# A macaron decoder layer on one Trainium2 core: four more raw slots for the paired products, low parts of w_out on VectorE, the residual through GpSimd's queue

## The chip, the cores and the metric

The kernel runs on one NeuronCore of a Trainium2 chip. The metric is the device time of one execution in microseconds; less is better. A program's matrix products run on TensorE (PE; its weight loads are listed as PEld), elementwise work on VectorE (DVE), ScalarE (ACT) and GpSimd (POOL). Transfers are issued by instructions in the order of an engine's queue: here SyncE (SP) issues most of them, and GpSimd those that add to what lies at the target or that gather. All run on the core's 16 DMA engines.

## The reference

One decoder layer in float32 on 512 prompt tokens and 8 x 4 sample tokens (544 columns), model width 1024, hidden width 2816. Two half-step feed-forward networks (FFNs) enclose a mixer with attention heads and recurrent heads; `project`, `moba_*` and `hgrn2_chunked` are left out here, as the change touches none of their work:

```python
def swiglu(x, w_gate, w_up, w_down):
    return (jax.nn.silu(x @ w_gate) * (x @ w_up)) @ w_down
...
        yp = yp + 0.5 * swiglu(rms_norm(yp, ffn1_norm[l]), ffn1_gate[l], ffn1_up[l], ffn1_down[l])
...
        qa, ka, va, qb, kb, ib, lf, gb = project(rms_norm(yp, mix_norm[l]), w_in[l], q_norm[l],
                                                 k_norm[l], lower_bounds[l])
        attn = moba_prompt(qa, ka, va, rel_bias_table)
        rec, s_fin = hgrn2_chunked(qb, kb, ib, lf, s0)
        yp = yp + merge_groups(attn, rec, gb, hgrn_out_norm[l], w_out[l])
...
        yp = yp + 0.5 * swiglu(rms_norm(yp, ffn2_norm[l]), ffn2_gate[l], ffn2_up[l], ffn2_down[l])
```

The sample tokens take the same path with caches of keys, values and states.

## The kernel before

**Split products.** Activations lie transposed, eight tiles of 128 model rows by 544 columns, which are worked on in two halves of 272. Each float32 factor is split into a high part in TensorE's format fp32r and a low part, the difference; a product is three matrix products (high by high, high by low, low by high) added up in PSUM (`products`, line 702). One output tile of 128 rows is a column; a plain column with 8 row tiles has 8 x 2 x 3 = 48 matrix products.

**Weights.** `weight_jobs` (504) lists all weight columns in the order in which they are used: ffn1, w_in, w_out, ffn2. A plain column is loaded in two parts of 128x512 (256 KB). `w_load` (583) gives each source the next free raw slot (`room`, 552) and issues its load on SP; there are four raw slots, tile `raw`. `w_split` (620) makes high and low part in one of six weight slots (`whi`, `wlo`) and gives the raw slot back. `split_unit` (608) has two ways for the low part: ScalarE's cast for the high part and a subtraction on VectorE, or, with `transfer`, a second pass of ScalarE that writes the source negated and rounded and an accumulating transfer on GpSimd's queue that adds the source onto it and reads the raw slot until it has landed. The transfer way is used for all of w_in and w_out (the job's flag `mixer`) and for the second part of the first five gate and up columns of an FFN. `w_pump` (662) splits up to 4 units ahead, 6 where the job has the flag `mixer`.

**Paired columns.** From column f = 5 on (`NREG`, 53), gate and up of an FFN are made together by seven products in place of eight (`paired_gemm` 739, `hidden_paired` 905): 7 units x 4 row tiles x 3 = 84 matrix products. The job has five sources: half of gate, half of up, their sum (made by GpSimd in a raw slot, no load), the other half of up and the other half of gate; the second half of up is also added onto the first by an accumulating transfer. Each unit is split like a plain one. The evacuations between the products run on ScalarE and VectorE, among them ScalarE's copies into `t_g` and `sq`. At column 5, `ffn` (960) adds ten raw slots and three weight slots for paired columns by `more_slots` (568): the tiles xh0 to xl4, which hold the split activations of the plain columns until then.

**From the mixer to ffn2.** `mix` (1835) ends with the first two columns of w_out, in four PSUM buffers. `ffn2` (1902) opens a new memory pool where the mixer's was, loads the residual from DRAM into its eight tiles y (1907), adds the two columns that are made and makes the other six by `gemm` (712), which has three PSUM buffers of the kind `mm`; an addition to y gives a buffer back. `norm_add` (815) then squares and sums y, on GpSimd for tiles 1 to 6.

**What sets the order.** The order of each engine's instructions is written by a planner at build time (`Order`, 258): it gives every instruction a planned start from costs of its own and sorts by it. Instructions that are recorded before a pool closes come ahead of those recorded after. On the chip each engine takes its instructions in this order and waits where an operand isn't ready. All are recorded through one helper, so that every row of the trace bears line 288; tiles tell them apart.

Of the kernel before, what the change touches and what calls it, by code (L numbers as in the profile page):

```python
# [21 lines left out]
KD = D // 128  # L22
# [28 lines left out]
MIXED = (4, 5, 6, 0, 1, 2, 3, 7)  # L51
OVER, TICK, WARM_COLUMNS = 0.0112, 3.413, 3060
NREG = 5
AHEAD = 4
AHEAD_MIX = 6
PACE = 1.1
# [408 lines left out]
class Build:  # L465
# [38 lines left out]
    def weight_jobs(self):  # L504
        a, out = self.a, []

        def quarters(m, nk, r0, c0):
            h = nk // 2
            return [m[128 * r:128 * (r + h), c0:c0 + 128].rearrange("(k p) m -> p k m", p=128)
                    for r in (r0, r0 + h)]  # L510

        def turns(m, nk, r0, c0):
            rows = m[128 * r0:128 * (r0 + nk), c0:c0 + 128].rearrange("(k two p) m -> two p k m", two=2, p=128)
            return [rows[0], rows[1]]

        def job(kind, src, nk):
            out.append({"kind": kind, "src": src, "nk": nk // 2, "raw": [], "done": 0, "paired": kind is not None, "mixer": False})

        def plain(m, nk, r0, c0, mixer=False, start=False):
            job(None, quarters(m, nk, r0, c0), nk)  # L520
            out[-1]["mixer"] = mixer
            out[-1]["start"] = start

        def paired(kind, nk, a11, a12, a21, a22, transfer):
            job(kind, [a11, a21, a21 if transfer else None, a22, a12], nk)
            out[-1]["transfer"] = transfer

        def ffn(p, pairs):
            gate, up, down = (a[p + n][0] for n in ("_gate", "_up", "_down"))
            for g0, ng in FGROUPS[pairs]:  # L530
                for f in range(g0, g0 + ng):
                    if f < NREG:
                        plain(gate, KD, 0, 128 * f, start=True)
                        plain(up, KD, 0, 128 * f, start=True)
                    else:
                        paired("a", KD, *quarters(gate, KD, 0, 128 * f), *quarters(up, KD, 0, 128 * f), pairs)
                for m in range(0, KD, 2):
                    if pairs:
                        paired("a", ng, *turns(down, ng, g0, 128 * m), *turns(down, ng, g0, 128 * (m + 1)), True)
                    else:  # L540
                        plain(down, ng, g0, 128 * m)
                        plain(down, ng, g0, 128 * (m + 1))

        ffn("ffn1", False)
        for n, j in IN_ORDER:
            plain(a["w_in"][0], KD, 0, COLS[n] + 128 * j, True)
        for m in range(KD):
            plain(a["w_out"][0], KD, 0, 128 * m, True)
        ffn("ffn2", False)
        return out  # L550

# [110 lines left out]
    def w_pump(self):  # L662
        def ahead():
            mixer = self.splitting < len(self.jobs) and self.jobs[self.splitting]["mixer"]
            return len(self.units) < (AHEAD_MIX if mixer else AHEAD)

# [293 lines left out]
    def ffn(self, pool, wide, home, x, xg, done, pairs, first=None):  # L960
        nc = self.nc
        self.pairs, self.sums, self.hidden_raw = pairs, wide, (pool, "t_h")
        for g0, ng in FGROUPS[pairs]:
            last = g0 + ng == NFF
            hs = []
            for f in range(g0, g0 + ng):
                if f >= NREG:
                    if f == NREG:
                        yield from self.settle()
                        yield lambda: len(self.xw) == KD // 2  # L970
                        self.more_slots("a", home, [f"{t}{i}" for i in range(5) for t in ("xh", "xl")],
                                        [(f"xh{i}", f"xl{i}") for i in range(5, KD)])
                        self.w_pump()
                    yield from self.paired_gemm(self.xw, KD // 2, self.hidden_paired(pool, f - g0, hs))
                    continue
                gate, up = self.hidden(pool, f - g0, hs)
                if f == 0 and first:
                    for evac, src in zip((gate, up), first):
                        for h in range(2):
                            self.later.append(lambda e=evac, s=src, h=h: e(s[h], h))  # L980
                    continue
                yield from self.gemm(xg, KD, gate, both=f == 0)
                yield from self.gemm(xg, KD, up)
            if pairs:
                for m in range(0, KD, 2):
                    yield from self.paired_gemm(hs, ng // 2, self.down_paired(pool, x, m, done if last else lambda m: None))
                continue
            yield from self.settle()
            if last:
                self.fewer_slots()  # L990
            for m in range(KD):

                def add(p, h, m=m, last=last):
                    c = self.cols(h)
                    nc.vector.scalar_tensor_tensor(x[m][:, c], p, 0.5, x[m][:, c], op0=ALU.mult, op1=ALU.add)
                    if h and last:
                        done(m)

                yield from self.gemm(hs, ng, add, both=m == 0)
        if pairs:  # L1000
            self.fewer_slots()
# [900 lines left out]
    def ffn2(self, xspill):  # L1902
        nc = self.nc
        with self.pool("ffn2") as pool:
            x = [pool.tile([128, T], F32, name=f"y{k}") for k in range(KD)]
            for k in range(KD):
                nc.sync.dma_start(x[k], xspill[k])
            xg = []
            for m in range(KD):

                def add(p, h, m=m):
                    c = self.cols(h)
                    nc.vector.tensor_tensor(x[m][:, c], p, x[m][:, c], op=ALU.add)
                    if h:
                        xg.append(self.split_x(x[m], m, self.gains[:, 2, m:m + 1], pool))
                        self.norm_add(m, x[m])

                if m < 2:
                    for h in range(2):
                        add(self.wo[m][1][h][:, :HT], h)  # L1920
                else:
                    yield from self.gemm(self.mixed, KD, add, self.mix_order)
            self.R = None
            self.order.spawn(self.norm())
            out = self.o["y_prompt"][0].rearrange("(i p) d -> p i d", p=128)
            out_s = self.o["y_sample"].rearrange("b t d -> (b t) d")

            def store(m):
                yield
                y = self.tl(pool, [128, 4, 128], "yt", bufs=2)  # L1930
                ys = self.tl(pool, [NS, 128], "t_s", bufs=2)
                self.to_tokens(x[m], y, ys)
                nc.sync.dma_start(out[:, :, 128 * m:128 * m + 128], y)
                nc.sync.dma_start(out_s[:, 128 * m:128 * m + 128], ys)
                self.stored += 1

            self.stored = 0
            homes = [(self.xp, f"{t}{i}") for i in range(KD) for t in ("xh", "xl")] + [(pool, f"hw{i}") for i in range(5)]
            self.hidden_home, self.staging = lambda i: homes[i], 12
            self.order.spawn(self.right_factors(pool, x, 2))  # L1940
            yield from self.ffn(pool, pool, pool, x, xg, lambda m: self.order.spawn(store(m)), False)
            yield lambda: self.stored == KD
# [41 lines left out]
```

## Time and profile before

| | |
|---|---|
| median of 3 runs | 1221.71 us |
| lowest and highest | 1219.51, 1222.38 us |
| the profiled execution | 1219.56 us |
| its span, first to last instruction | 1217.8 us |
| TensorE busy | 1180.5 us, 97% of the span |
| VectorE, ScalarE, GpSimd busy | 780.5, 600.8, 281.8 us |
| bytes moved | 177.26 MB, 146 GB/s on the mean |

Where ffn1 lies is about 0 to 402 us, the mixer to 781, ffn2 with the rest of w_out behind it. In the rows an instruction reads: start, duration, engine, line, operation, output<-inputs, shapes, count; in brackets how long its engine had been idle and what ended that. An engine ending in q is its queue for transfers. Matmul records are pipelined, so neighbours overlap; the time of a column is read from start to start.

### The profile page before, as it was taken

How to read it: one execution, taken by the hardware profiler on the slowest of the kernel's cores; microseconds unless marked ns; L12 is line 12 of the kernel's file. 1: busy time of each engine (PE TensorE's matmuls, PEld its weight loads, DVE VectorE, ACT ScalarE, POOL GpSimd, SP SyncE). 2: the span in 40 equal slices, each digit the busy share in tenths (PEclk: the TensorE clock that was granted, in tenths of full speed). 3: DMA queues.
4: the chain of work that ended last, by engine and by line, in shares of the span. 5: the costliest groups of instructions: out<-in, count | busy, mean ns of one | idle time of the engine just before them, and what ended most of it. 6: DMA issues, size and time to landing. Idle time of an engine off the chain costs nothing.

```text
span 1217.8 us, 26505 instructions
## 1 busy us (share of the span) xinstructions
PE 1180.5 (97%) x10571; PEld 1117.7 (92%) x10571; DVE 780.5 (64%) x1662; ACT 600.8 (49%) x1223; POOL 281.8 (23%) x293
## 2 busy tenths in 40 slices
PE   8999999999999989999999999699989999999998
PEld 8989999999999988889888777599989999999998
DVE  5888458854775377875675357237767478845853
ACT  6645246532555446666556533255544255514642
POOL 4121021101103541213354446141110011101000
PEclk9999999999999989999999999799989999999999
DMA  6566444453325984755787988565455334533232
GB/s 171 130 168 161 127 134 120 124 139 79 87 66 153 223 214 116 174 122 133 225 230 205 277 282 272 124 158 120 118 153 157 86 87 122 142 102 87 53 110 69
DMA packets 234607, 177.26 MB, mean 146 GB/s; under 512 B 14019, under 2 KB 206051, under 8 KB 234484
## 3 DMA queue, kind: packets, MB, share of 16 engines
q1 hardware_dynamic: 206740, 108.83, 30.8%
q0 software_dynamic: 27648, 66.60, 23.8%
q8 instruction: 83, 1.36, 0.5%
q14 instruction: 40, 0.33, 0.1%
q10 hardware_dynamic: 96, 0.14, 0.0%
HBM read 133.94 MB, written 11.83 MB: 120 GB/s over the span
## 4 chain that ended last, share of the span: by engine, by line
PE 85%; DVE 5%; DMA 4%; issue 3%; ACT 1%; POOL 1%; SPq 0%; POOLq 0%; ACTq 0%; DVEq 0%
PE mm L288 58%; PE sm L288 27%; DMA wlo<-raw 1%; DMA raw<-ffn_gate 1%; DMA raw<-w_in 1%; DMA SC<-rsample 0%; DMA xin<-x_prompt 0%; DVE ms_qk L288 0%; DVE wlo L288 0%; DVE xl L288 0%; SPq L288 0%; POOL wlo L288 0%; DVE t_qk L288 0%; ACT sq L288 0%; POOL KV L288 0%
## 5 line engine op out<-in xcount | busy, mean ns | idle before, releaser
L288 PE MATMUL mm<-xh,whi 128*128 128x272 f32 x1216 | 364.5, 300 | 11.1 <-DVE y L288 9.2
L288 PE MATMUL mm<-xl,whi 128*128 128x272 f32 x1216 | 352.6, 290 | 2.0 <-DVE xl L288 1.9
L288 PE MATMUL mm<-xh,wlo 128*128 128x272 f32 x1216 | 352.5, 290 | 0.1
L288 ACT CAST whi<-raw 128x512 fp32r<-128x512 f32 (+1 forms) x256 | 154.5, 606 | 224.5 <-PE mm L288 160.5
L288 PEld LDWEIGHTS mm<-xh,whi 128*128 128x128 f32 x1216 | 231.6, 190 | 26.8 <-issue 13.6
L288 PEld LDWEIGHTS mm<-xl,whi 128*128 128x128 f32 x1216 | 231.3, 190 | 3.1 <-DVE xl L288 3.0
L288 PEld LDWEIGHTS mm<-xh,wlo 128*128 128x128 f32 x1216 | 231.1, 190 | 0.4 <-issue 0.4
L288 DVE TENSOR_TENSOR wlo<-raw,whi 128x512 fp32r<-128x512 f32 (+1 forms) x166 | 113.4, 690 | 61.9 <-ACT whi L288 59.1
L288 PE MATMUL mm<-hw,whi 128*128 128x272 f32 x704 | 132.3, 288 | 0.0
L288 POOL DMA_DIRECT2D wlo<-raw x90 | 81.3, 931 | 218.2 <-ACT wlo L288 181.8
L288 PE MATMUL sm<-xw,whi 128*128 128x272 f32 x648 | 124.3, 290 | 0.4 <-ACT t_g L288 0.4
L288 PE MATMUL mm<-xw,whi 128*128 128x272 f32 x648 | 123.2, 288 | 0.8 <-ACT t_g L288 0.8
L288 PEld LDWEIGHTS mm<-hw,whi 128*128 128x128 f32 x704 | 110.2, 188 | 0.2 <-issue 0.2
L288 PEld LDWEIGHTS sm<-xw,whi 128*128 128x128 f32 x648 | 102.8, 190 | 0.6 <-ACT t_g L288 0.6
L288 PEld LDWEIGHTS mm<-xw,whi 128*128 128x128 f32 x648 | 101.9, 189 | 1.0 <-ACT t_g L288 1.0
L288 PE MATMUL mm<-hw,wlo 128*128 128x272 f32 x352 | 101.2, 287 | 0.0
L288 PE MATMUL sm<-xw,wlo 128*128 128x272 f32 x324 | 94.0, 290 | 0.0
L288 PE MATMUL mm<-xw,wlo 128*128 128x272 f32 x324 | 93.3, 288 | 0.0
L288 PEld LDWEIGHTS mm<-hw,wlo 128*128 128x128 f32 x352 | 66.3, 188 | 0.0
L288 PE MATMUL sm<-xw,xh 128*128 128x272 f32 x304 | 60.6, 295 | 3.0 <-ACT sq L288 3.0
L288 PEld LDWEIGHTS sm<-xw,wlo 128*128 128x128 f32 x324 | 61.7, 190 | 0.2
L288 PE MATMUL mm<-xw,xh 128*128 128x272 f32 x304 | 59.7, 292 | 2.1 <-ACT sq L288 2.1
(324 smaller groups left out, 2163.4 us busy)
## 6 DMA issues: line engine op xcount, KB each, us to landing
wlo<-raw POOLq DMA_DIRECT2D x90, 256.0 KB, 4.0
raw<-ffn_down SPq DMA_DIRECT2D x64, 256.0 KB
raw<-w_in SPq DMA_DIRECT2D x56, 256.0 KB
raw<-ffn_gate SPq DMA_DIRECT2D x38, 256.0 KB
raw<-ffn_up SPq DMA_DIRECT2D x36, 256.0 KB
xl<-ffn_up SPq DMA_DIRECT2D x28, 256.0 KB
xh<-ffn_gate SPq DMA_DIRECT2D x26, 256.0 KB
xh<-ffn_up SPq DMA_DIRECT2D x24, 256.0 KB
```

The lines of the kernel that those rows point to most:

```text
L288: call(*map(real, args), **{k: real(v) for k, v in kw.items()})
```

## The change

Three edits. At the beginning of each FFN, four raw slots (`rawx0` to `rawx3`) are added that only paired jobs can take; they lie in ffn1's pool `wide` and in ffn2's own pool and stay until the ten others are given up too. The eight w_out columns lose the flag `mixer`: their 16 low parts are made by VectorE's subtraction, and the units that may be split ahead while they are next are 4, not 6. The eight residual loads are issued on GpSimd's queue, not SP's.

```diff
@@ -51,6 +51,7 @@
 NREG = 5
+NX = 4
 AHEAD = 4
@@ -545,7 +546,7 @@
         for m in range(KD):
-            plain(a["w_out"][0], KD, 0, 128 * m, True)
+            plain(a["w_out"][0], KD, 0, 128 * m)
         ffn("ffn2", False)
@@ -960,6 +961,7 @@
     def ffn(self, pool, wide, home, x, xg, done, pairs, first=None):
         nc = self.nc
         self.pairs, self.sums, self.hidden_raw = pairs, wide, (pool, "t_h")
+        self.more_slots("a", wide, [f"rawx{i}" for i in range(NX)], [])
         for g0, ng in FGROUPS[pairs]:
@@ -1904,7 +1906,7 @@
             for k in range(KD):
-                nc.sync.dma_start(x[k], xspill[k])
+                nc.gpsimd.dma_start(x[k], xspill[k])
             xg = []
```

## Rows read from the trace of the kernel before

**Rows 1.** The page, part 1: busy us, share, instructions of each engine

```profile
PE 1180.5 (97%) x10571; PEld 1117.7 (92%) x10571; DVE 780.5 (64%) x1662; ACT 600.8 (49%) x1223; POOL 281.8 (23%) x293
```

**Rows 2.** Waits of PE, whole span: total us, times, longest us

```profile
PE mm L288 <- DVE y L288: 9.2, 1, 9.2
PE sm L288 <- ACT sq L288: 3.0, 1, 3.0
...
PE mm L288 <- ACT sq L288: 2.1, 1, 2.1
```

**Rows 3.** The chain that ended last: start us, us, what

```profile
83.40 3.96 DMA raw<-ffn_gate
...
166.42 10.55 PE sm L288 x84
...
891.87 5.59 DMA raw<-ffn_gate
```

**Rows 4.** Stretches: us, busy us of PE, PEld, DVE, ACT, POOL, granted clock, DMA

```profile
78.87:94.81 15.94, 12.89 (x86) 11.99 (x85) 10.34 (x15) 7.51 (x16) 4.33 (x4) 0.89 0.81 218
720.00:755.00 35.00, 34.48 (x653) 28.79 (x647) 25.32 (x74) 18.04 (x52) 21.09 (x22) 1.00 0.90 269
755.00:771.20 16.20, 11.89 (x114) 9.26 (x113) 12.31 (x33) 3.23 (x6) 0.90 (x1) 0.79 0.38 126
781.11:795.57 14.46, 5.31 (x26) 5.15 (x25) 3.41 (x7) 2.80 (x5) 1.01 (x1) 0.65 0.86 241
888.45:907.71 19.26, 15.34 (x87) 14.43 (x86) 10.81 (x16) 7.42 (x16) 4.32 (x4) 0.74 0.79 202
```

**Rows 5.** SP's queue from 780 to 900 in order of time

```profile
779.95 5.63 SPq L288 DMA_DIRECT2D raw<-w_out  x3
785.87 4.25 SPq L288 DMA_DIRECT2D y<-xs  x8
```

**Rows 6.** Waits of SP's queue from 770 to 800: total us, times, longest us

```profile
SPq L288 <- DMA wlo<-raw: 31.8, 5, 14.2
```

**Rows 7.** GpSimd and VectorE from 770 to 800 in order of time

```profile
775.11 0.99 POOL L288 DMA_DIRECT2D wlo<-raw  x1 [19.22 <-ACT wlo L288]
...
779.35 1.73 POOL L288 DMA_DIRECT2D wlo<-raw  x2 [1.85 <-ACT whi L288]
794.56 1.40 POOL L288 TENSOR_TENSOR sqsum<-sqsum,sq 128x544 f32<-128x544 f32 x1 [13.47 <-ACT sq L288]
...
770.38 0.72 DVE L288 TENSOR_TENSOR xl<-rec,xh 128x544 fp32r<-128x544 f32 x1
```

**Rows 8.** Instructions on tile wlo: count, ns min/median/max, first and last start

```profile
L288 DVE TENSOR_TENSOR wlo<-raw,whi x166: 557/684/1692, 8.9 to 1198.1; 128x512 fp32r<-128x512 f32 x134, 128x384 fp32r<-128x384 f32 x32
...
L288 POOL DMA_DIRECT2D wlo<-raw x90: 851/874/1502, 25.3 to 874.2; - x90
```

**Rows 9.** Instructions on tile y, in the same form

```profile
L288 DVE TENSOR_TENSOR y<-mm,y x14: 430/441/443, 789.9 to 826.0; 128x272 f32<-128x272 f32 x14
L288 SPq DMA_DIRECT2D y<-xs x8: 339/431/749, 785.9 to 789.4; - x8
```

**Rows 10.** The page, part 6: DMA issues, KB each, median us to landing

```profile
wlo<-raw POOLq DMA_DIRECT2D x90, 256.0 KB, 4.0
```

**Rows 11.** Groups of GpSimd's instructions from 720 to 755: busy us, mean ns, idle before

```profile
L288 POOL DMA_DIRECT2D wlo<-raw x6 | 5.6, 941 | 7.3 <-ACT wlo L288 7.1 <-issue 0.2
```

**Rows 12.** SP's queue before the first paired columns of ffn1 and ffn2

```profile
58.72 0.38 SPq L288 DMA_DIRECT2D raw<-ffn_up  x1
...
78.67 0.37 SPq L288 DMA_DIRECT2D raw<-ffn_gate  x1
...
862.10 2.59 SPq L288 DMA_DIRECT2D raw<-ffn_up  x2
```

**Rows 13.** ScalarE in the first paired column of ffn2

```profile
897.54 0.62 ACT L288 CAST whi<-raw 128x512 fp32r<-128x512 f32 x1 [4.05 <-DMA raw<-ffn_gate]
```

**Rows 14.** GpSimd ahead of the first paired column of ffn1

```profile
69.87 1.86 POOL L288 TENSOR_TENSOR raw<-raw,raw 128x512 f32<-128x512 f32 x1 [3.61 <-DVE wlo L288]
```

## The prediction, made before the changed kernel ran

> **What bounds the kernel now.** I read the page first, then who TensorE waited for, then a table of stretches around those waits, then the queues behind them. By the page TensorE is busy for 1180.5 of 1217.8 us, 97% [rows 1]. So the kernel is bound by TensorE's products, and an edit away from TensorE pays only where TensorE stands still, or where its clock is low because it stood still. There are few such places. Of all its waits the longest is one of 9.2 us on the residual tile y, and next stand one of 3.0 us and one of 2.1 us, both on ScalarE's copy into sq [rows 2].
>
> The stretches give what each place costs. A paired column is 84 products and takes 10.55 us where nothing disturbs it [rows 3], 0.1256 us a product. The first paired column of ffn1 takes from 78.87 to 94.81, 15.94 us, which is 5.4 us too long (call it place A). That of ffn2 takes from 888.45 to 907.71, 19.26 us, 8.7 us too long (place B); the granted clock is 0.74 on its mean, so a good part of it ran at the lower of TensorE's two levels (1.2 of 2.4 GHz), which came behind the 3.0 us wait [rows 4]. The second half of output column 2 of w_out takes from 781.11 to 795.57, 14.46 us for 24 products that need 24 x 0.1256 = 3.0 us: 11.4 us too long (place C); its clock is 0.65 on the mean, behind the 9.2 us wait [rows 4]. Together 25.5 us, about all that the changed lines can reach.
>
> **Place C: the y loads and w_out.** TensorE needs a PSUM buffer that VectorE frees by adding y0, so y0's landing ends the stall. The eight loads y<-xs stand on SP's queue behind three loads of w_out sources that need 5.63 us, and go out at 785.87 [rows 5]. Why those are late: in this stretch SP waits five times, 31.8 us in all, on DMA wlo<-raw, the accumulating transfer that makes a low part and holds its source until it has landed [rows 6]. What y0 itself needs is the mixer's memory. The mixer's last VectorE instruction is xl<-rec at 770.38, over at 771.1 [rows 7]: SP's queue costs y0 about 14.8 us.
>
> After the change y0 stands on GpSimd's queue. In the kernel before GpSimd has been idle for 19.22 us when it issues wlo<-raw at 775.11; three more such issues follow, the last two at 779.35, and then nothing until 794.56 [rows 7]. The second part of the change takes just these four away. So I place the first issue at about 771.2. An issue by GpSimd takes 0.874 us at the median [rows 8], one on SP took 0.431 [rows 9]; the nearest price for the way from issue to landing is the 4.0 us of wlo<-raw, 256 KB against y's 272 [rows 10]. y0 lands at 771.2 + 0.9 + 4.0 = 776.1, and two additions of 0.441 us [rows 9] end at 777. TensorE wants the buffer at 781.1. This leaves 4 us, and more if y0 waits only for the tile whose place it takes and not for the whole mixer's memory. y1 to y7 follow at 0.9 us each, faster than a column of 48 products (6.0 us) uses them. Behind the loads on GpSimd wait the sums of squares (the one at 794.56 and five like it); nobody needs these before the norm. All 11.4 us go: bounds 9.2 (the wait alone, the slow clock staying) to 11.4, and I take 11.3, as TensorE then meets no wait before a fall of the clock.
>
> By the Trainium skill (DMA: Bandwidth & Descriptors, section Issuing engines are not separate DMA queues) the issuing engine does not matter, as all transfers run on the same 16 engines and only issue time is saved. The trace here shows another thing, a transfer stuck behind waiting ones on the same queue; by that rule place C would give nothing and the sum below 12.1 us for 23.4 (the second rival has its time).
>
> The w_out low parts: 16 pairs of a ScalarE pass and a GpSimd issue become 16 subtractions on VectorE at 0.684 us [rows 8]. Ten of them lie from 775 on. There VectorE had nothing to do from 771.1 to 789.9, and later a column of 6.0 us holds two additions (0.88 us), the split of y and now two subtractions (1.37 us): nothing on the path. The sources come free 0.68 us after the cast rather than after a pass, an issue and a landing of 4.0 us, so SP's next loads go out earlier. The other six stand from 720 to 755 [rows 11], beside the last recurrent head, whose steps keep VectorE busy for 25.32 of 35 us there and for 12.31 of the next 16.2 us [rows 4]. At worst all six delay that chain: 6 x 0.684 = 4.1 us. At best gaps take them, and GpSimd's cache gathers, which stand between the six issues of 0.941 us, end sooner by two of these, a gain of 1.9. Between -1.9 and 4.1 I take a loss of 1.0, near the middle, as VectorE's share there, 0.72, lies between free and full. If the waiting limit for units ahead falls from 6 to 4, six weight slots with two in use leave four anyhow: nothing.
>
> **Places A and B: four more raw slots.** A paired column needs five sources. Before the change it has the four ordinary slots, and the ten further ones (xh, xl) are inputs of the last plain product and free only as TensorE passes it. In ffn1 the last source of a plain column goes out at 58.72, and in ffn2 the last two by 864.69, but in ffn1 the fifth source of the first paired column only at 78.67 [rows 12], and the first source of the second paired column at 83.40. The chain that ended last runs through this very load, and in ffn2 through the one at 891.87, which took 5.59 us [rows 3]. ScalarE takes its instructions in order: its cast at 897.54 waited 4.05 us for that load [rows 13], and behind it in its order stands the copy into sq, for which TensorE waits [rows 2].
>
> With the change the first four sources go to the new slots, unused so far, directly behind the last plain load: about 59 in ffn1, about 865 in ffn2. GpSimd's sum for this column, which takes no load but a slot, waits until 69.87 for a plain split to give one back [rows 14]; so by about 70 the ordinary slots of ffn1 are free again, and by the same pattern by about 877 those of ffn2, and they take the fifth source and the second column's first three. TensorE asks for the first column at 78.87 and 888.45 and for the second 10.55 us later: against landings of 4 to 5.6 us the loads are ahead by 9 us or more. The sums on GpSimd and its accumulating transfer per column move with them, in the same number; ahead of them in GpSimd's order stand the low parts of the last plain column, which could lose one issue (0.9 us) and have 3 us to spare. The work on ScalarE and VectorE is the same and holds in every later paired column at 10.55 us. What is late next is a cast that waits for a weight slot, as in any column. I leave 0.5 us at each place for a short wait without a fall of the clock: 4.9 us at A and 8.2 at B. Bounds: nothing (the wait only moves to the next source) and all 5.4 and 8.7. The rest of each FFN runs at full pace already, and gains nothing.
>
> **The sum.** 11.3 + 4.9 + 8.2 - 1.0 = 23.4 us. The profiled execution took 1219.56 us (span 1217.8); this gives 1196.2. The median of the runs shown, 1221.71, is 2.1 us above it, so I forecast 1198.3, with 1191 to 1204 as its own range: the order of the mixer's instructions is laid out anew by the planner, and I allow 4 us either way, which no row prices, besides the bounds above.
>
> **The rivals.** First: the paired columns wait still. ScalarE's order is fixed beforehand, and a cast that waits there for any late source holds the copies again; the clock falls after short waits too (0.89 on the mean at A, with waits of 2.1 and less [rows 2, 4]). For it speaks that the planner's place for a cast rests on planned landings; against it the lead of 9 us. Half of 13.1 us stays: 1204.9. Chance 0.16.
>
> Second: y still comes late, since GpSimd's queue is held by something that I don't see or the mixer's memory is given back as a whole later than 771.1. A and B stay: 1198.3 + 11.3 = 1209.6. Against it stands GpSimd's empty queue. Chance 0.09.
>
> Third: the new slots are not used early, as loads are issued in a planned order, and C also stays: 1218 to 1222, chance 0.05.
>
> Fourth, slower: VectorE becomes the bound of the mixer's end. The six subtractions go between the recurrent head's steps, TensorE gets waits of about 3 us there, and its clock falls as it does behind the 3.0 us wait of place B. From 720 to 755 it now works nearly without a gap, 34.48 of 35 us at a clock of 1.00 [rows 4]; at the lower level this is up to 34 us more, and 1198.3 + 34 = 1232. [...] Chance 0.04.
>
> **How the numbers follow.** Forecast 0.64; better than its range 0.02. Differences of 0.3%, 3.7 us, are about what a measurement of this kernel tells from none. Faster: 0.64 + 0.02 + 0.16 + 0.09 = 0.91; same 0.05; slower 0.04. The range 1190 to 1208 holds the forecast, the first rival and a little of the second, some 0.83.
>
> **What would show it.** TensorE's list of waits without the 9.2 us on y and without sq; y<-xs issued by GpSimd within a microsecond or two of the mixer's last VectorE instruction; the fifth gate source issued some 10 us before the first paired column starts; both such columns near 10.6 us with a clock of 1.00. Wrong would be a wait of y on another queue, a cast waiting for raw<-ffn_gate in those columns, or new gaps of TensorE between the last heads.

## The result, and the profile after

The changed kernel takes 1205.64 us (1204.40 to 1207.49) where the kernel before takes 1222.05 us (1219.51 to 1223.85) beside it: ratio 0.9868, 95% interval 0.9845 to 0.9892, so 13 to 19 us less. It is faster, by 16.4 us of the medians, and 7 us above the forecast of 1198.3: inside the range of 1190 to 1208 that took in the first rival, outside the forecast's own of 1191 to 1204. Its profiled execution took 1206.72 us (span 1204.9), 12.84 us less than that of before (1219.56), where the sum had 23.4.

Who TensorE waited for in the changed kernel over the whole span (total us, times, longest us), as in [rows 2]; its rows bear line 289:

```profile
PE sm L289 <- issue: 4.0, 11, 0.8
PE mm L289 <- DVE xl L289: 3.8, 3, 2.2
...
PE mm L289 <- ACT sq L289: 2.1, 1, 2.1
...
PE mm L289 <- DVE t_h L289: 1.5, 2, 1.2
...
PE mm L289 <- DVE wlo L289: 1.3, 1, 1.3
```

The 9.2 us on y and the 3.0 us on sq are gone; there is still one of 2.1 us on sq, in the same column as before (place A). The stretches of the changed kernel say the same (columns as in [rows 4]): the first and the second paired column of ffn1, from its last paired column through the mixer to column 2 of w_out, from there to the first paired column of ffn2, and that column:

```profile
80.77:97.20 16.43, 12.76 (x87) 12.14 (x85) 12.82 (x17) 6.67 (x14) 6.57 (x6) 0.90 0.90 228
97.20:108.94 11.74, 11.26 (x86) 10.67 (x85) 10.40 (x20) 8.06 (x17) 0.00 (x0) 1.00 0.45 118
354.50:785.32 430.82, 416.46 (x4582) 358.64 (x4581) 272.10 (x728) 225.50 (x512) 157.69 (x174) 0.99 0.69 188
785.32:883.97 98.65, 98.59 (x791) 98.37 (x789) 68.79 (x144) 50.87 (x90) 21.41 (x21) 1.00 0.54 139
883.97:894.51 10.54, 10.54 (x86) 10.54 (x85) 8.52 (x13) 6.97 (x15) 4.79 (x4) 1.00 1.14 292
```

With the same stretches of before the account of the two profiled executions is:

| stretch | before | after | change | forecast |
|---|---|---|---|---|
| start of the first paired column of ffn1 | 78.87 | 80.77 | +1.90 | |
| that column (place A) | 15.94 | 16.43 | +0.49 | |
| the second one | 10.66 | 11.74 | +1.08 | |
| from the third to the last of ffn1 | 245.98 | 245.56 | -0.42 | A in all: -4.9, came +3.05 |
| mixer, to column 2 of w_out | 426.65 | 430.82 | +4.17 | +1.0 |
| to the first paired column of ffn2 (C) | 110.35 | 98.65 | -11.70 | -11.3 |
| that column and the next (B) | 29.85 | 21.39 | -8.46 | -8.2 |

So places B and C came in the size that was forecast, place A became a loss, and the mixer got longer. These two differences, 8.0 and 3.2 us, are what is missing.

**Where place A went.** SP's queue and GpSimd of the changed kernel in the plain columns of ffn1, in order of time:

```profile
32.06 0.45 SPq L289 DMA_DIRECT2D rawx<-ffn_gate  x1
32.56 1.05 SPq L289 DMA_DIRECT2D rawx<-ffn_up  x2
...
44.58 0.38 SPq L289 DMA_DIRECT2D raw<-ffn_gate  x1
```

```profile
37.08 1.87 POOL L289 TENSOR_TENSOR rawx<-rawx,rawx 128x512 f32<-128x512 f32 x1 [9.46 <-DMA rawx<-ffn_up]
...
40.06 2.06 POOL L289 DMA_DIRECT2D wlo<-raw  x2
```

The sources of column 5 go out at 32 us, in the middle of the plain columns, not at 59. GpSimd takes its instructions in order, so its sum waits 9.46 us for these loads, and behind it stand two low parts of a plain column; their raw slots come free late, the gate load behind them goes out at 44.58 (the same load in the kernel before, in the row below, at 38.02), and TensorE waits 1.33 us for a low part at 50.83; by the first paired column it is 1.9 us behind.

```profile
38.02 0.38 SPq L288 DMA_DIRECT2D raw<-ffn_gate  x1
```

The code says why 32 us: the planner gives a tile that was never used the opening of its pool as its earliest time (`self.order.touched[name] = self.since`, line 176), and puts its load into the first gap of SP's plan.

In the first paired column itself, the second cause, on SP's queue, ScalarE and TensorE:

```profile
83.64 1.36 SPq L289 DMA_DIRECT2D rawx<-ffn_up  x1
```

```profile
89.46 0.62 ACT L289 CAST whi<-rawx 128x512 fp32r<-128x512 f32 x1 [4.72 <-DMA rawx<-ffn_up]
89.98 0.38 ACT L289 COPY sq<-mm 128x272 f32<-128x272 f32 x1
```

```profile
90.41 0.52 PE L289 MATMUL mm<-xw,xh 128*128 128x272 f32 x2 [2.14 <-ACT sq L289]
```

A source of the second column was given an extra slot that comes free late; its load stands behind eight loads into the tiles xh and xl (a column has four loads) and goes out at 83.64, the cast waits 4.72 us for it, and the copy into sq behind the cast holds TensorE for 2.14 us. It is the picture of [rows 13], with the next source. The column is 5.9 us too long; 1.5 us more are waits on VectorE's t_h, and the granted clock is 0.90 on its mean.

### The profile page after: what moved, and what is told of

It is laid out like the page before. It is cut to its first block, busy times and chain, and to the rows that moved or that the text cites. A ratio compares the mean times of both kernels' runs of the same rounds, so it can differ in the third digit from the quotient of the medians.

```text
span 1204.9 us, 26484 instructions
## 1 busy us (share of the span) xinstructions
PE 1175.7 (98%) x10571; PEld 1112.3 (92%) x10571; DVE 793.0 (66%) x1678; ACT 593.4 (49%) x1207; POOL 270.6 (22%) x285
## 4 chain that ended last, share of the span: by engine, by line
PE 84%; DVE 5%; DMA 4%; ACT 2%; issue 2%; POOL 2%; SPq 0%; POOLq 0%; ACTq 0%; DVEq 0%
PE mm L289 57%; PE sm L289 27%; DMA SC<-rsample 1%; DMA rawx<-ffn_up 1%; DMA wlo<-raw 1%; DMA xl<-ffn_up 1%; ACT xh L289 1%; DVE wlo L289 1%; ACT sq L289 1%; DMA xin<-x_prompt 0%; POOL sqsum L289 0%; ACT whi L289 0%; DVE xl L289 0%; DMA raw<-w_in 0%; DVE raw L289 0%
## 5 line engine op out<-in xcount | busy, mean ns | idle before, releaser
L289 ACT CAST whi<-raw 128x512 fp32r<-128x512 f32 (+1 forms) x242 | 146.0, 605 | 225.2 <-PE mm L289 176.6
L289 DVE TENSOR_TENSOR wlo<-raw,whi 128x512 fp32r<-128x512 f32 (+1 forms) x168 | 116.7, 700 | 57.7 <-ACT whi L289 55.1
L289 POOL DMA_DIRECT2D wlo<-raw x74 | 67.1, 936 | 175.7 <-ACT wlo L289 141.4
L289 PEld LDWEIGHTS mm<-xw,wlo 128*128 128x128 f32 x324 | 61.0, 188 | 0.0
```

Source lines behind the costliest of these rows:

```text
L289: call(*map(real, args), **{k: real(v) for k, v in kw.items()})
```

## The experiments

The kernels ran on several chips, on which the kernel before has medians of 1218.6 to 1224.6 us; so times are compared by their ratio to the kernel before on the same chip, and stretches, which are sharper, by the profiles. Several edits work on loads of ffn1 alone, whose job numbers are below 60 (`self.loading`); number 10 is the first paired column.

**The slots in ffn2 alone**

```diff
-        self.more_slots("a", wide, [f"rawx{i}" for i in range(NX)], [])
+        if pool is wide:
+            self.more_slots("a", wide, [f"rawx{i}" for i in range(NX)], [])
```

> The change, but with the four extra slots opened in ffn2 alone. Theory (in ffn1 the slots themselves cost time): the 3.05 us by which ffn1 ended later than before come back, the first paired column of ffn1 takes 15.9 us again from about 78.9, the first w_out product of column 2 starts at about 782.4 in place of 785.49, ffn2 keeps its 10.5 us column, and the time is 1205.6 - 3.05 = 1202.6. Rival (the mixer's end lost its 4.3 us only because ffn1 fell 3 us behind): that comes back as well, 1198.3. Second rival (all of it is the planner's chance and has nothing to do with the slots in ffn1): 1205 to 1206.

Median 1203.54, ratio 0.9881 (0.9839 to 0.9923), its profiled execution 1199.73. Stretches, first two paired columns of ffn1 and the mixer:

```profile
79.72:96.06 16.34, 12.02 (x86) 10.79 (x85) 11.53 (x17) 7.67 (x16) 4.33 (x4) 1.00 0.79 213
96.06:106.73 10.67, 10.67 (x86) 10.58 (x85) 9.63 (x17) 7.36 (x16) 2.66 (x2) 1.00 0.59 126
352.71:778.43 425.72, 413.47 (x4582) 357.66 (x4581) 271.21 (x728) 225.58 (x512) 157.18 (x174) 0.99 0.70 191
```

ffn1 gives back 2.2 us (third column at 106.73, not 108.94), and the mixer another 5.1. The time cannot tell the theory from the second rival; the stretches can: the slots cost time in ffn1. The first rival's mixer came back too; but the kernel without any extra slots, below, has the old ffn1 as well and the longest mixer of all, 434.23 us, so ffn1 does not decide it. Over all profiles the third paired column starts at 105.47 to 107.59 us in the four with the old ffn1 (mean 106.55) and at 108.19 to 109.68 in the five with the early fill (mean 108.97): a loss of 2.4 us. It has the same sign on each of three chips: 106.73 against 109.68, 107.59 against 108.64 and 109.41, 106.40 against 108.19.

**A later fill, and a later fill for one column only.** The first edit moves the loads of the first paired column behind the last plain gate load, the second also keeps the extra slots of ffn1 to its first paired column:

```diff
+        if x["extra"] and raw.name not in self.order.before and self.loading < 60:
+            self.order.touched[raw.name] = self.order.free["pe"] + 10
```

```diff
+        if self.loading < 60 and self.loading != 10:
+            free = [x for x in free if x["tags"][0][:4] != "rawx"]
```

> The change, but in ffn1 a slot that was never filled gets as its earliest planned time TensorE's time at that point plus 10 us, so that the four sources of the first paired column are issued behind the last plain gate load, not at 32 us. Theory (two causes in ffn1, each with its place): the early issue blocks GpSimd's low parts and costs the 1.9 us by which the first paired column started late, and these come back (start 78.9); the second cause, the source of the second paired column that waits in a late slot, stays, as its load still stands behind those of the third column: first column about 16, third column's start about 107 in place of 108.94; 1205.6 - 1.9 = 1203.7. Rival (the early issue is harmless, and the late start has another cause): start 80.8, 1205 to 1206. Second rival (the early issue was the only cause): first column 10.6 to 11, 1205.6 - 3.05 - 4.9 = 1197.7.

> As the kernel with the late fill, and in ffn1 only the first paired column may take the extra slots, so that no source of the second one waits for such a slot. Theory (both causes together make up place A): the first paired column starts at 78.9 and takes 10.6 to 12 us, ffn1 ends 3.05 + 4 us earlier than in the changed kernel, and the time is about 1198.5. Rival (the wait moves on again, to the second column's sources, which now wait for the ten later slots as they did before): the first column is short, but the second one takes 13 us or more and the gain against the changed kernel is 3 to 4 us, 1202. Second rival (the cast waits for something else): no gain beyond that of the late fill, 1203.7.

Late fill: 1199.94, ratio 0.9843 (0.9800 to 0.9886). Loads at 65.41; the first column starts at 79.79 and takes 15.49, the third starts at 106.25 (107 was expected). So about half of the 1.9 us came back, not all: with the old ffn1 the first paired column starts at 79.02 on the mean of four profiles, with the early fill at 80.89 on that of five. The time is below the expected 1203.7 because the mixer took 426.61 us here, 4.2 less than in the changed kernel's profile. The second cause is still on ScalarE of this kernel, while TensorE's wait behind it is shorter than the 2.1 us of the changed kernel:

```profile
89.03 0.62 ACT L289 CAST whi<-rawx 128x512 fp32r<-128x512 f32 x1 [4.49 <-DMA rawx<-ffn_up]
```

```profile
PE mm L289 <- ACT sq L289: 0.4, 1, 0.4
```

For one column only: 1200.16, ratio 0.9854 (0.9814 to 0.9894). Stretches of its first two paired columns, and its mixer:

```profile
80.27:93.98 13.71, 11.41 (x87) 10.70 (x85) 13.14 (x20) 8.04 (x18) 4.46 (x4) 1.00 0.75 189
93.98:104.49 10.51, 10.51 (x87) 10.51 (x86) 8.62 (x17) 6.94 (x15) 0.88 (x1) 1.00 0.68 172
350.24:775.56 425.32, 412.46 (x4583) 356.54 (x4581) 271.64 (x728) 225.60 (x512) 156.88 (x174) 0.99 0.70 191
```

The wait on the load is gone, the second column runs at full pace and the third starts at 104.49, 1.8 us before that of the late fill. So both causes were real and the wait did not move on; but the first column stays 3 us above its full pace, where 10.6 to 12 us were expected. VectorE is busy for 13.14 of its 13.71 us, and TensorE's longest waits from 70 to 108 us are on what VectorE makes:

```profile
PE mm L289 <- DVE wlo L289: 1.4, 2, 0.8
PE mm L289 <- DVE t_h L289: 1.2, 1, 1.2
```

One reason stands just ahead of it, on VectorE and GpSimd of this kernel:

```profile
72.36 1.78 DVE L289 TENSOR_TENSOR wlo<-raw,whi 128x512 fp32r<-128x512 f32 x1
...
74.53 1.87 DVE L289 SCALAR_TENSOR_TENSOR hw<-hw,hw 128x272 f32<-128x272 f32 x1
```

```profile
72.18 1.41 POOL L289 TENSOR_TENSOR rawx<-rawx,rawx 128x512 f32<-128x512 f32 x1 [6.19 <-issue]
...
74.49 1.60 POOL L289 TENSOR_TENSOR raw<-raw,raw 128x512 f32<-128x512 f32 x1
```

Two instructions of VectorE last 1.1 to 1.4 us longer than elsewhere (0.684 in [rows 8]; 0.44 for the second form elsewhere in the trace), each while a sum of GpSimd runs. The Trainium skill (SBUF — State Buffer, section SBUF: two separate sides) has the two engines share a pair of ports that one holds for a whole instruction; the trace agrees in these two, which end at 74.14 and 76.40, 0.5 and 0.3 us after the sums (73.59 and 76.09). That VectorE's load is what keeps the 3 us was read from these waits, not tested.

**The low parts of w_out as before**

```diff
-            plain(a["w_out"][0], KD, 0, 128 * m)
+            plain(a["w_out"][0], KD, 0, 128 * m, True)
```

> The change with its second part undone: the low parts of w_out come by ScalarE's pass and GpSimd's accumulating transfer again. Theory (VectorE's subtractions cost the mixer's end its 4.3 us, and the empty queue of GpSimd is what lets y come early): the mixer's end is 3 to 4 us shorter (column 2 of w_out starts at about 781.5 to 782.5), but four low parts stand ahead of the first y load on GpSimd's queue, y0 is issued at about 784 and lands at about 788, and TensorE waits 3 to 5 us for it and has a slow clock behind it: 1205.6 - 4 + 6 = 1207 to 1209. Rival (the mixer's end was lost to the planner's new order and not to VectorE): column 2 starts at 785 or later and y comes 3 us late as well, 1209 to 1212. Second rival (y's queue was all that mattered): the wait on y is under 1 us and the time 1201 to 1202.

Median 1211.71, ratio 0.9943 (0.9922 to 0.9965): the second part is worth some 9 us (8 to 9 by the ratios of the changed kernel, 0.9868 and 0.988), more than was expected. GpSimd's queue, and TensorE's wait and stretch behind it:

```profile
782.64 1.74 POOL L289 DMA_DIRECT2D wlo<-raw  x2 [1.85 <-ACT whi L289]
783.97 4.22 POOL L289 DMA_DIRECT2D y<-xs  x7
```

```profile
PE mm L289 <- DVE y L289: 6.7, 2, 6.2
```

```profile
781.38:889.09 107.71, 100.93 (x790) 100.27 (x789) 62.82 (x136) 54.68 (x98) 32.29 (x36) 0.97 0.65 156
```

The theory holds in its order (four low parts, then y at 783.97) and is too small in its size: the stretch is 9.06 us longer than with VectorE's low parts. The mixer takes 426.14 us here.

**y on SP's queue again**

```diff
-                nc.gpsimd.dma_start(x[k], xspill[k])
+                nc.sync.dma_start(x[k], xspill[k])
```

> The change with its third part undone: the eight residual loads on SP's queue again, with the low parts of w_out on VectorE. Theory (the waiting loads of w_out ahead of y on SP's queue were what made y late, and VectorE's low parts have taken most of that wait away): y goes out about 3 us later than on GpSimd's queue, TensorE waits 1 to 3 us for it and has some slow clock behind; from column 2 of w_out to the first paired column of ffn2 it takes 101 to 104 us in place of 98.65, and the whole 2 to 5 us more than the changed kernel. Rival (the rule that the issuing engine does not matter, the low parts did all): 98.5 to 99 us, and no difference in time. Second rival (the queue did nearly all): 107 us or more, as without the low parts on VectorE.

Median 1208.49, ratio 0.9876 (0.9845 to 0.9908), against 0.988 (0.9843 to 0.9917) for the changed kernel beside it. SP's queue, TensorE's one wait on y, the stretch:

```profile
780.22 1.87 SPq L289 DMA_DIRECT2D raw<-w_out  x2
782.51 3.67 SPq L289 DMA_DIRECT2D y<-xs  x8
```

```profile
PE mm L289 <- DVE y L289: 0.5, 1, 0.5
```

```profile
783.28:882.85 99.57, 99.05 (x790) 98.60 (x789) 69.19 (x144) 50.77 (x90) 21.65 (x20) 1.00 0.54 141
```

My theory falls: y goes out some 3 us later relative to column 2, as it said, but this costs 0.92 us, and the times cannot be told apart, which is nearest to the rival that the low parts did all. SP's waits for wlo from 770 to 800 us are 10.9 us here, on VectorE, where they were 31.8 us on the transfer [rows 6]. Together with the run above, place C splits as follows (us from column 2 of w_out to the first paired column of ffn2; the last entry lies between 98.63 and 98.66 in all ten profiles with both parts, among them the one without extra slots, so the slots don't matter here):

| | y on SP | y on GpSimd |
|---|---|---|
| low parts by transfer | 110.35, 109.58 | 107.71 |
| low parts on VectorE | 99.57 | 98.65 |

**No extra slots at all** (the line of the first edit taken out)

> The change without its first part: no extra slots in either FFN. Theory (the slots in ffn2 are worth place B): the first paired column of ffn2 takes 18 to 19.5 us again and its time is 8.2 us above that of the kernel with the slots in ffn2 alone (1203.5 median, 1199.7 in its profile): 1208 to 1212. Rival (with the earlier y and the low parts of w_out the loads of ffn2 are ahead anyhow): the column takes 10.5 to 13 us, and the time is within 3 us of that kernel's.

Median 1214.47, ratio 0.9911 (0.9876 to 0.9946), 6.3 us above the changed kernel on the same chip. The first paired column of ffn2, and ScalarE in it:

```profile
886.52:903.30 16.78, 11.54 (x87) 10.74 (x85) 9.98 (x14) 6.50 (x15) 4.32 (x4) 1.00 0.81 203
```

```profile
895.42 0.62 ACT L289 CAST whi<-raw 128x512 fp32r<-128x512 f32 x1 [3.20 <-DMA raw<-ffn_gate]
```

The waits on the gate loads are back (another is 3.48 us), the column is 6.2 us too long (8.7 and 7.6 in the two profiles of before, where the granted clock is lower than the 1.00 here): less than the theory said, and clearly not the rival. The slots make place B.

**The fill later still** (plus 20 in place of plus 10, one column)

> As the kernel with the late fill for one paired column of ffn1, with the four sources 10 us later still, behind the last plain load of all. In that kernel the first paired column takes 13.71 us, and VectorE is busy for 15.17 of the 16 us from 80 on. Theory (what is left of place A is VectorE's own work, which the time of the loads does not change): 13 to 14.5 us, and the time within 1 us of that kernel's. Rival (it is still GpSimd's sums and loads that come at a wrong time): the column takes under 12 us or over 15 us, and the time moves by 2 us with it.

Median 1210.88, ratio 0.9893 (0.9862 to 0.9925). TensorE's wait, ScalarE, and the column:

```profile
PE mm L289 <- ACT whi L289: 5.3, 1, 5.3
```

```profile
85.77 0.62 ACT L289 CAST whi<-rawx 128x512 fp32r<-128x512 f32 x1 [2.81 <-DMA rawx<-rawx]
```

```profile
79.15:98.25 19.10, 12.89 (x86) 12.22 (x85) 14.35 (x23) 9.49 (x18) 6.00 (x6) 0.82 0.80 196
```

My theory falls and the rival's marks come: the loads at 72 us are too late for the accumulating transfer that needs two of them, and the column takes 19.10 us. From a fill at 65 us to one at 72 us the column grows by 5.4 us. Since the loads themselves went wrong here, the run does not test what VectorE's work costs. The first paired column starts at 79.15, so this fill does give the late start back.

**Between the two** (plus 0, one column), on one chip with the late fill, the changed kernel and the kernel before:

> As the kernel with the late fill for one paired column, with the four sources 10 us earlier, between the loads of the last two plain columns. The fill at 32 us stood ahead of low parts on GpSimd's queue, the one at 72 us came too late for the transfer that adds two sources (it landed at about 85 us and TensorE waited 5.3 us for the cast behind it). Theory (between these there is a time that harms neither): the first paired column takes 10.6 to 13 us and starts by 80.3 us, third column at 101.5 to 104.5 us. Rival (GpSimd's sum, wherever it stands among the low parts of the plain columns, delays them): the plain columns lose 1 us or more (start at 81 us or later) and the third column comes at 105 us or later.

> The kernel with the late fill for one paired column again, beside the changed kernel on one chip. Theory (the fill at about 65 us is a better time than the one at 32 us, and the one column keeps the second column free of the wait): third paired column at 104 to 105.5 us, 4 to 5 us ahead of the changed kernel, and as much less time. Rival (its gain was the other chip's): within 2 us of the changed kernel.

> The changed kernel, with a profile on the same chip as the kernel before. Theory and rival for the mixer as there. For ffn1, theory (the early fill of the extra slots costs 2 to 3 us there): the third paired column starts at 108.5 to 109.7 us, against 105.5 to 107.6 in the kernel before; rival (that was the execution too): within 1 us of each other.

| | median us | ratio, interval | third paired column |
|---|---|---|---|
| changed | 1207.50 | 0.9868 (0.9836 to 0.9900) | 108.19 |
| late fill, one column | 1203.04 | 0.9838 (0.9813 to 0.9863) | 103.76 |
| fill between, one column | 1202.12 | 0.9828 (0.9801 to 0.9854) | 105.12 |

The kernel before has its third column at 106.40 there. So the early fill costs 1.8 us there (2 to 3 were expected), and the late one for one column gains 2.6 against before and 4.4 against the changed kernel, where the medians differ by 4.5. The fill between starts at 80.25 and keeps a first column of 14.33 us: it is neither the quiet place that the theory hoped for nor the loss of the rival, and its time cannot be told from the late one's. Both beat the changed kernel by medians; the intervals still touch.

**The mixer**

> The changed kernel once more, unaltered, beside the kernels below on one chip. In the profile the mixer of the changed kernel lasted 4.2 us longer than with the late fill, although from the end of ffn1 on every engine has the same instructions in the same order in both. Theory (the execution or the chip of that profile did it, not the change): from the last paired column of ffn1 to column 2 of w_out it takes 425.5 to 427 us, as in the four other kernels, in place of 430.8, and the profiled execution comes out at about 1202. Rival (the shift in ffn1 moves the mixer against its gathers and so costs 4 us each time): 430 to 431.5 us again, and 1205 to 1207.

> The kernel before, unaltered, with a profile on the same chip as the kernels below. Profiles of kernels whose instructions stand in the same order on every engine from the end of ffn1 on gave 426.6 us (late fill) and 432.7 us (the change once more, on another chip) for the stretch from the last paired column of ffn1 to column 2 of w_out, and the long ones show 3 to 4.5 us of short stops of TensorE put down to issue, the short ones none. Theory (the chip or the execution sets this, not the change): the kernel before and the changed kernel on one chip lie within 2 us of each other in this stretch, both near 426 or both near 431 us. Rival (the change costs the mixer 4 us): the kernel before stays at 426 to 427 us and the changed one is 4 us longer.

The changed kernel once more: 1208.16, ratio 0.988 (0.9843 to 0.9917), mixer 432.68. Its stretch on the chip of the last runs, and those of the kernel before and of the late fill for one column beside it:

```profile
353.74:786.81 433.07, 418.22 (x4582) 359.65 (x4581) 273.40 (x728) 225.53 (x512) 158.20 (x174) 0.99 0.69 187
```

```profile
352.37:780.08 427.71, 415.18 (x4583) 357.81 (x4581) 267.08 (x719) 230.03 (x521) 161.69 (x174) 0.99 0.71 192
```

```profile
349.38:781.96 432.58, 417.58 (x4583) 359.87 (x4581) 272.25 (x728) 225.90 (x512) 158.40 (x174) 0.99 0.69 187
```

The last kernel is the one that took 425.32 us above, unaltered: 7.3 us between two executions of one program. TensorE's waits on issue in this stretch, in that kernel here, in the kernel before here, and in that kernel on the other chip:

```profile
PE sm L289 <- issue: 4.3, 10, 0.8
PE mm L289 <- issue: 1.8, 1, 1.8
```

```profile
PE sm L288 <- issue: 3.1, 9, 0.5
```

```profile
PE mm L289 <- issue: 0.6, 1, 0.6
```

Neither theory of the first run holds alone; between the kernel before and the changed one on one chip the rival holds, 427.71 against 433.07. With low parts on VectorE the mixer takes 425.3 to 426.6 us in the three profiles that have under 1 us of waits on issue, and 428.3 to 434.2 in the eight that have 3.8 to 6.1 us of them; with the low parts by transfer 426.1 to 427.7, with such waits or without. So the 4.2 us are no fixed price of VectorE's subtractions, but where the stops occur the changed kernels lose some 5 us more than the kernel before. As far as the chip is on record, the stops go with it: the four profiles of one chip (the slots in ffn2 alone, the two kernels with the late fill, w_out's low parts by transfer) have 0.2 to 0.9 us of them, the eight on two other chips 3.3 to 6.1.

Part of the loss can be placed. The kernel before reaches the 3800th product of this stretch at 722.63 us, about where its first low part of w_out goes out (721.74). Up to there TensorE's products come in the same order in the kernels of this table (us, counted along the products in the traces):

| | to the 3800th product | from there to column 2 |
|---|---|---|
| before | 371.18 | 55.47 |
| changed | 372.37 | 58.45 |
| first chip: low parts by transfer | 370.72 | 55.42 |
| first chip: on VectorE, three kernels | 369.33 to 371.14 | 55.47 to 55.99 |
| last chip: before | 371.21 | 56.50 |
| last chip: on VectorE, three kernels | 373.38 to 374.56 | 58.02 to 59.45 |

So 1.19 of the 4.17 us came ahead of w_out's low parts, where the change touches nothing in the mixer, and 2.98 beside them; there VectorE's low parts came with 0.05 to 0.57 us more on the first chip and 1.5 to 3.0 on the last. Why the stops come and why the rest differs is open.

## Why the prediction was right and where it was wrong

The direction and the wide range (1190 to 1208) held; the forecast of 1198.3 with its own range to 1204 did not. TensorE's few long waits were the right place to look: the three stretches moved, and the rest of either FFN by under 0.5 us. (One wait was overlooked in the list: behind the 3.0 us the next longest is one of 2.5 us on kt in the mixer, which the change does not reach.)

**Place C, right in size (11.3, measured 11.70), wrong in its cause.** "SP's queue costs y0 about 14.8 us" gave the gain to the queue. By the table of place C the queue alone gives 1.9 to 2.6 us, the low parts on VectorE alone 10.0 to 10.8. What held SP's queue were loads that wait for DMA wlo<-raw [rows 6], and the second part ends these waits on SP as it empties GpSimd; either queue then is early enough. The marks came: no wait on y at place C, y issued at 781.27, 0.6 us behind the mixer's last split, as VectorE's and GpSimd's rows show:

```profile
779.93 0.72 DVE L289 TENSOR_TENSOR xl<-rec,xh 128x544 fp32r<-128x544 f32 x1
```

```profile
781.27 4.37 POOL L289 DMA_DIRECT2D y<-xs  x8 [21.67 <-PE mm L289]
```

But what released the issue was a product of TensorE, not that split, and the first two additions end at 787.44, about 0.9 us before TensorE asks for the buffer (3.0 us into column 2, which starts at 785.32), where the prediction had a lead of 4. An issue took 0.558 us, not 0.874. The rule of the Trainium skill (DMA: Bandwidth & Descriptors, section Issuing engines are not separate DMA queues) fits the lower row of that table, 0.92 us, and leaves out what the upper row has, a queue of waiting instructions. The prediction's 12.1 us by that rule left out that the second part also empties SP's queue: alone it gives 10.0 us or more of place C.

**Place B, right in size** (8.2, measured 8.46). The loads did not go out "about 865" there either, but at the opening of ffn2's pool, 784.55. This did no harm: GpSimd's sum stood behind a sum of squares and did not wait for the loads, and what follows it, an accumulating transfer of the same column and more sums of squares, TensorE does not need soon; the column took 10.54 us.

```profile
784.55 0.37 SPq L289 DMA_DIRECT2D rawx<-ffn_gate  x1
```

```profile
800.78 1.29 POOL L289 TENSOR_TENSOR rawx<-rawx,rawx 128x512 f32<-128x512 f32 x1
```

**Place A, wrong by 8 us.** The step that failed is "the first four sources go to the new slots, unused so far, directly behind the last plain load: about 59 in ffn1". I took the time from when the loads are wanted, where the planner goes by when the tile is allowed, and its code was there to be read. The sentence on GpSimd ("low parts of the last plain column, which could lose one issue") named the right queue and priced the wrong wait: it is the wait for the load, 9.46 us, that the low parts stand behind. And "the fifth source and the second column's first three" left out its fourth: that is the first rival, which came true here and not at B. That the time lies within 1 us of its 1204.9 is luck: it had half of A and B staying, where all of A stayed, none of B did and the mixer added 3 us.

**The mixer, wrong by 3 us.** +1.0 became +4.17 in that profile and -1.3 to +7.6 across the profiles, against 426.65; the bounds of -1.9 to 4.1 with 4 more for the planner held the first value. In the part of the mixer where the six subtractions stand the loss was 2.98 us in that profile and 0.05 to 3.0 in comparisons on one chip, within the bounds without the planner's 4. No run separates the subtractions from the new order that comes with them.

**The sum.** 8.0 from A and 3.2 from the mixer less 0.7 at B and C are the 10.5 us between 23.4 and 12.9.

## What to carry to other kernels

A buffer that is always free let this planner put a load into the first gap of the queue, and whatever an in-order engine does with that load goes out of order with it: find the instructions behind the consumer, and give the load an earliest time. When two edits both take away one wait, run each alone before giving either the credit. A stretch that holds many short products should be compared over several executions before a few microseconds of it are put down to a change.

## What the runs showed of the hardware

One program's mixer took 425.32 us on one chip and 432.58 on another, with 6.1 us of waits on issue in the long one and 0.6 in the short one; of the eleven stops in the long one six sit at products with results of 128x16, but the longest, 1.80 us, at one of 128x272. Two of VectorE's instructions, which take 0.44 and 0.68 us elsewhere, lasted 1.8 to 1.9 us while GpSimd added two tiles. A plain load issued by GpSimd took 0.558 us, against 0.874 for an accumulating one and 0.431 for a load issued by SP [rows 8, 9].
